# A pooling layer's channel product in three 16-bit products, with its weights in the common stream

## The chip, the cores and the metric

The kernel runs on one core of a Trainium2 chip. The metric is the device time of one execution in microseconds (us). Three runs of the kernel before gave 2080.56, 2081.57 and 2083.05 us, median 2081.57. The profiled execution took 2081.02 us, of which the span from the first to the last instruction is 2079.2 us.

The engines are called as the profile calls them: PE (matmul), PEld (weight load for PE), DVE (vector), ACT (scalar and activation), POOL, and SP (which issues nearly all DMA transfers). Each engine works through its own list of instructions in order, and waits where an instruction needs what another engine has not yet delivered.

## The reference, cut to what matters

Two layers work on 256 tokens of 2048 channels in 32-bit floats. Each layer has a token mixer and a gated FFN with a short convolution; each of the two is framed by RMS norms with shift, scale and gate. The mixer of layer 0 is a state-space layer with a GLU, that of layer 1 is a pooling mixer:

```python
def _pool_mixer(u, w, scale):
    ...
    for g, win in enumerate(POOL_WINDOWS):      # windows of 2, 4, 8, 16 tokens
        ...                                     # groups: 512 channels each
        groups.append((cs[:, hi + 1] - cs[:, lo]) / cnt - uf[:, :, ch])
    p = jnp.stack(groups, axis=2).astype(u.dtype)
    y = jnp.einsum("blgc,gcd->blgd", p, w).reshape(bsz, n_tok, dim)
    return y * scale
```

So each of four groups of 512 channels is averaged over a window of tokens (less the token itself) and multiplied by a matrix of 512 by 512. Both steps are linear, so that the kernel may multiply by the matrix first and pool afterwards.

## The kernel before, in words

Activations lie channel-major: `x` is 16 tiles of 128 channels by 256 tokens. The big products (GLU, FFN up, FFN down) are each made of three products of 16-bit halves, `hi*vh + hi*vl + lo*vh`, 256 tokens at a time. Their weights come as a stream of pieces of 128 by 2048 floats (`stream`, `self.pieces`). `load` brings piece q into one of three buffers `st`; `high` makes its 16-bit high part times 128 (`WS`) on ACT (`WH<-st` in the profile, L74); `ensure` then makes the low part on DVE (`XW<-st,WH`, L70), and issues the next load. High and low parts stand in a ring of four slots. I call high and low of one piece together a split. During the FFN, `after` keeps the splits three pieces ahead of the products. The order of every engine's work is that in which the Python code emits it.

Layer 1's mixer is emitted so. `norms(3)` sums the squares that the preceding FFN left and makes two row scales, `bc[0]` and `bc[1]`. `chain` then goes over the 16 tiles (two single ones, then seven pairs) on DVE: `op_t` scales the FFN's output (`Y<-Y,bc33bc`), `op_x` adds it to `x` (`XW<-XW,Y`), `op_r` scales `x` (`Z<-XW,mm33bc`), and ACT applies scale and shift. With `parted=False`, the pooling's call, the result stays a 32-bit tile `uf`; with `parted=True`, the FFN's call, ACT also writes the 16-bit high part and DVE, in `op_lo`, the low part (`Z<-u,Z`).

`pooling` works on four groups. `first(g)` multiplies tokens by the group's matrix: eight 32-bit products of 512 columns (`pp`), from weights that `pool_load` and one later transfer put into the buffer `G`; ACT copies the result out of PSUM. `second(g)` applies the pooling band (`py`, four output tiles of three small 32-bit products). For each output tile `sums` makes, on ACT, the scaled copy `Y<-py` and two squares `q<-py` and `q<-Y`, and on DVE a product `q<-Y,XW` and the running sum `G<-G,q` over 768 columns; there are three buffers `q`, and the last tile's sums are not added on DVE. The order is first(0), first(1), second(0), first(2), second(1), second(2), first(3), second(3). One piece of the stream is split meanwhile (`ensure(self.piece + 3)` after group 1); three more pieces, for the following FFN, have been split before the stage begins. `some()` slips in a little of a matrix-vector product (`gac`) for the conditioning.

Then `norms(3)` again, whose first matmuls (`pa`) need the running sum, and `ffn(1)`, whose first job `up_first` takes the tiles as `chain` delivers them (`pf`), the remaining jobs being `pu`.

Of the kernel before, what the change touches and what calls it, by code (L numbers as in the profile page):

```python
# [4 lines left out]
F32 = mybir.dt.float32  # L5
# [6 lines left out]
P = 128  # L12
# [33 lines left out]
class Net:  # L46
# [223 lines left out]
    def stream(self):  # L270
        A, half = self.A, lambda a: [a[:, :2048], a[:, 2048:]]
        self.pieces = []
        for i in range(NT):
            self.pieces += half(A["glu"][i])
        for l in range(2):
            a, b = half(A["up"][l, 0]), half(A["up"][l, 1])
            self.pieces += [a[0], b[0], a[1], b[1]]
            for i in range(2, NFF):
                self.pieces += half(A["up"][l, i])
            for j in range(NT):  # L280
                d = A["down"][l, j]
                self.pieces += [d[:, 0:2048], d[:, 2048:4096], d[:, 4096:5632]]
        self.piece = self.loaded = self.highs = self.lows = 0
        self.ring = [[t[:, i * 1024 : (i + 1) * 1024].bitcast(F16) for t in (self.WH, self.WL)] for i in range(4)]

        self.low0 = self.G[:, 10240:11264].bitcast(F16)
# [28 lines left out]
    def take(self):  # L315
        self.piece += 1
        return self.parts(self.piece - 1)[1:]
# [13 lines left out]
    def uh(self, k):  # L331
        return self.zh[k // 8][:, k % 8]
# [535 lines left out]
    def main(self):  # L868
        tc, nc, A = self.tc, self.nc, self.A
        par, con = self.par, self.con  # L870
        with tc.tile_pool(name="m1", bufs=1) as mp, tc.tile_pool(name="tm", bufs=2) as tm, tc.tile_pool(
# [10 lines left out]
            cvs = mp.tile([P, 2, 3, 88], F32, name="cvs")  # L882
            pcm = self.G[:, 11264 : 11264 + 8 * 4 + 8 * 64]
            load, high, ensure, take, prods, uh, ul = self.load, self.high, self.ensure, self.take, self.prods, self.uh, self.ul
            uf = self.Z.rearrange("p (k t) -> p k t", t=SEQ)

            cvf = cvs.rearrange("p l w t -> p (l w t)")
            nc.gpsimd.dma_start(pcm, A["pcm"])
# [217 lines left out]
                spread(1)  # L1106
                return bc

            def chain(bc, sh, parted=True):

                parts = [(0, 1), (1, 2)] + [(i, i + 2) for i in range(2, NT, 2)]
                tl = {}

                def op_t(a, b):
                    self.mul(ym[:, a:b], ym[:, a:b], bc[0][:, None, :].to_broadcast([P, b - a, SEQ]))

                def op_x(a, b):
                    self.add(x[:, a:b], x[:, a:b], ym[:, a:b])

                def op_r(a, b):  # L1120
                    t = uf[:, a:b]
                    if parted:
                        t = tl[a] = tm.tile([P, 2, SEQ], F32, tag="u", name=f"u{self.nq}_{a}", bufs=3)
                    self.mul(t[:, : b - a], x[:, a:b], bc[1][:, None, :].to_broadcast([P, b - a, SEQ]))
                    for i in range(a, b):
                        self.act(t[:, i - a], t[:, i - a], AF.Identity, vec[:, 1, i : i + 1], sh[:, i : i + 1])
                    if parted:
                        self.copy(self.zh[a // 8][:, a % 8 : a % 8 + b - a], t[:, : b - a])

                def op_lo(a, b):  # L1130
                    if not parted:
                        return
                    s = slice(a % 8, a % 8 + b - a)
                    self.sub(self.zl[a // 8][:, s], tl.pop(a)[:, : b - a], self.zh[a // 8][:, s])

                op_t(*parts[0])
                for s, ab in enumerate(parts):
                    op_x(*ab)
                    if s + 1 < len(parts):
                        op_t(*parts[s + 1])  # L1140
                    op_r(*ab)
                    if s:
                        op_lo(*parts[s - 1])
                        yield parts[s - 1][1]
                op_lo(*parts[-1])
                yield NT

# [88 lines left out]

            mem = [self.G[:, i * 2048 : (i + 1) * 2048] for i in range(5)]
            band = mem[3].rearrange("p (h g t) -> p h g t", h=2, g=4)
            wp = [mem[i].rearrange("p (k n) -> p k n", k=4) for i in (0, 1, 2, 1)]
            vts = [mem[i][:, j : j + 1024].rearrange("p (h n) -> p h n", h=2) for i in (4, 0) for j in (0, 1024)]  # L1240

            def pool_load():
                nc.sync.dma_start(mem[0], A["pool"][0])
                nc.sync.dma_start(mem[1], A["pool"][1])
                nc.sync.dma_start(mem[3], A["band"])
                nc.sync.dma_start(mem[2], A["pool"][2])

            def pooling(bc):
                need(8)
                self.mul(vec[:, 2], self.mod[:, 8, 0], par[:, Q_NG + 80 : Q_NG + 96])  # L1250
                self.mul(vec[:, 2], vec[:, 2], par[:, Q_PS : Q_PS + 16])
                out = chain(bc, self.mod[:, 6, 0], False)
                done = 0

                def ahead(n):
                    nonlocal done
                    while done < min(n, NT):
                        done = next(out)

                def first(g):  # L1260
                    ahead(4 * g + 4)
                    pv = [mps.tile([P, 512], F32, tag="mm", name=f"pp{g}_{h}") for h in range(2)]
                    for k in range(4):
                        for h in range(2):
                            self.mm(pv[h], uf[:, 4 * g + k, h * 128 : h * 128 + 128], wp[g][:, k], k == 0, k == 3)
                    if g == 1:
                        nc.sync.dma_start(mem[1], A["pool"][3])
                    ahead(8 if g == 0 else NT)
                    if g:
                        some()  # L1270
                        some()
                    if g == 1:
                        ensure(self.piece + 3)
                    for h in range(2):
                        self.copy(vts[g][:, h], pv[h])

                def second(g):
                    vt = vts[g]
                    for o in range(4):
                        ps = mps.tile([P, SEQ], F32, tag="mm", name=f"py{g}_{o}")  # L1280
                        for h, a, first, last in ((0, 120, True, False), (1, 120, False, True), (0, 0, True, True)):
                            t = slice(a, 256 if a else 120)
                            self.mm(ps[:, t], vt[:, h, o * 128 : o * 128 + 128], band[:, h, g, t], first, last)
                        i = g * 4 + o
                        fins.append(sums(3, i, ps, par[:, Q_PS + i : Q_PS + i + 1], vec[:, 2, i : i + 1], True))
                        if i < NT - 1:
                            step()

                first(0)
                first(1)  # L1290
                second(0)
                first(2)
                second(1)
                second(2)
                first(3)
                second(3)


            while self.loaded < self.lows + 3:
# [16 lines left out]
            scale(0, 2, 4)  # L1316
            bc = norms(4)
            ffn(0, bc, (1.4, 1.5))
            pool_load()
            need(7)  # L1320
            scale(1, 0, 1)
            bc = norms(3)
# [138 lines left out]
```

## Time and profile before

| | us |
|---|---|
| median of three runs | 2081.57 |
| profiled execution | 2081.02 |
| its span | 2079.2 |
| PE busy | 1907.9 (92%) |
| DVE busy | 1687.5 (81%) |
| ACT busy | 977.4 (47%) |
| pooling stage, from the chain's first DVE instruction to the norm's first `pa` | 46.88 |
| the norm behind it, `pa` to the first `pf` | 14.37 |
| `up_first` of layer 1, first `pf` to first `pu` | 24.07 |

A timeline row gives start, duration, engine, line, operation, output and inputs; in brackets stands how long the engine had been idle just before it, and which engine ended that. Durations overlap slightly, since an instruction begins before the one ahead of it has drained; the step from start to start is what a long row of instructions costs. The layer-1 pooling stage is only 2% of the span, so the averages of the whole page say little about it, and the rows below are taken from it.

### The profile page before, as it was taken

The page shows a single profiled execution, that of the slowest core. Times are in us where ns is not written, and L with a number is a line of the kernel's source. Part 1 is how long each engine was busy: PE and PEld are TensorE (multiplying, and loading weights), DVE is VectorE, ACT ScalarE, POOL GpSimd, SP SyncE. Part 2 cuts the span into 40 slices and gives each one's busy share as a digit, 9 for nine tenths or more (in the row PEclk, how much of TensorE's full clock was granted, in tenths as well). Part 3 has the DMA queues.
Part 4 walks back from the last instruction along what each step waited for, and adds up shares of the span by engine and source line. Part 5 has one row for each costly group of instructions (what it writes and reads, how often), then busy time and mean ns, then how long its engine had stood idle before and what let it go on. Part 6 is the DMA issues. An engine that isn't in the chain of part 4 may idle for free. (4 is left out here: it accounts for less than half of the span.)

```text
span 2079.2 us, 44155 instructions
## 1 busy us (share of the span) xinstructions
PE 1907.9 (92%) x19300; PEld 1624.0 (78%) x19300; DVE 1687.5 (81%) x2204; ACT 977.4 (47%) x1139; POOL 111.6 (5%) x129
## 2 busy tenths in 40 slices
PE   5773775799989999999999999889999999999998
PEld 3651552688878888888888888578888888888886
DVE  8799889699889999999998898878777766654444
ACT  2341651655555554554444443655545555543442
POOL 0440251200000000000000000000000000000000
PEclk9785897899989999999999999889999999999999
DMA  8565347599938999999999999327767656555652
GB/s 320 223 237 215 138 179 264 217 356 367 334 111 335 340 355 341 333 338 328 343 332 357 358 366 353 137 100 264 259 236 261 242 201 203 198 190 201 209 201 77
DMA packets 77585, 541.62 MB, mean 260 GB/s; under 512 B 8912, under 2 KB 9168, under 8 KB 16464
## 3 DMA queue, kind: packets, MB, share of 16 engines
q1 hardware_dynamic: 74304, 526.06, 69.1%
q0 software_dynamic: 3088, 12.74, 1.6%
q8 instruction: 151, 2.47, 0.5%
q14 instruction: 42, 0.34, 0.0%
HBM read 536.67 MB, written 2.10 MB: 259 GB/s over the span
## 5 line engine op out<-in xcount | busy, mean ns | idle before, releaser
L82 PEld LDWEIGHTS <-WH 128*128 128x128 f16 x9472 | 927.3, 98 | 118.7 <-issue 9.5
L70 DVE SCALAR_TENSOR_TENSOR XW<-st,WH 128x2048 f16<-128x2048 f32 (+1 forms) x303 | 676.2, 2233 | 276.3 <-ACT WH L74 275.8
L74 ACT ACTIVATE WH<-st 128x2048 f16<-128x2048 f32 (+1 forms) x304 | 566.7, 1865 | 704.8 <-PE pu L82 364.4
L82 PE MATMUL pu<-Z,WH 128*128 128x256 f16 x5376 | 881.2, 273 | 0.0
L82 PE MATMUL pu<-Z,XW 128*128 128x256 f16 x2688 | 732.7, 273 | 0.0
L82 PEld LDWEIGHTS <-XW 128*128 128x128 f16 x4720 | 462.6, 98 | 59.6 <-issue 3.4
L82 PE MATMUL pd<-G,WH 128*128 128x256 f16 x2816 | 461.8, 273 | 0.2 <-DVE G L52 0.2
L82 PE MATMUL pd<-G,XW 128*128 128x256 f16 x1408 | 383.8, 273 | 0.0
L70 DVE SCALAR_TENSOR_TENSOR gac<-ra,cpad,gac 128x1024 f32<-128x1024 f32 x128 | 163.9, 1280 | 3.2 <-DMA ra<-ada 1.8
L82 PE MATMUL pg<-Z,WH 128*128 128x256 f16 x960 | 157.5, 273 | 0.0
L70 DVE SCALAR_TENSOR_TENSOR gac<-st,cpad,gac 128x1024 f32<-128x1024 f32 x112 | 143.4, 1281 | 7.3 <-DMA st<-ada 5.8
L70 DVE SCALAR_TENSOR_TENSOR hc<-pu,cvs,hc 128x255 f32<-128x255 f32 x336 | 138.6, 475 | 0.6 <-ACT hc L76 0.6
L82 PE MATMUL pg<-Z,XW 128*128 128x256 f16 x480 | 130.8, 273 | 1.6 <-DVE XW L70 1.6
L82 PE MATMUL gv<-st,cpad 128*32 128x128 f32 (+2 forms) x1024 | 87.7, 476 | 45.4 <-DMA st<-ada 45.4
L82 PEld LDWEIGHTS gv<-st,cpad 128*32 128x32 f32 x1024 | 30.9, 128 | 76.5 <-DMA st<-ada 60.7
L76 ACT ACTIVATE hc<-pu,par,cvs 128x256 f32<-128x256 f32 x168 | 84.3, 551 | 8.0 <-DVE G L52 8.0
L82 PE MATMUL y<-G,QX 128*32 128x128 f32 x768 | 32.0, 302 | 39.1 <-ACT QX L74 37.9
L82 PEld LDWEIGHTS y<-G,QX 128*32 128x32 f32 x768 | 23.9, 122 | 42.5 <-ACT QX L74 39.4
L52 DVE TENSOR_TENSOR G<-G,q 128x768 f32<-128x768 f32 (+2 forms) x56 | 49.8, 890 | 5.5 <-ACT q L74 3.6
L74 ACT ACTIVATE QX<-XW 64x512 f32<-64x512 f32 x32 | 35.7, 1116 | 36.3 <-DVE XW L52 30.3
L82 PE MATMUL pf<-Z,WH 128*128 128x256 f16 x256 | 47.7, 291 | 5.4 <-ACT Z L74 3.2
L74 ACT ACTIVATE hc<-hc 128x256 f32<-128x256 f32 x88 | 35.6, 405 | 27.7 <-DVE hc L70 26.4
(231 smaller groups left out, 1511.9 us busy)
## 6 DMA issues: line engine op xcount, KB each, us to landing
st<-up SPq DMA_DIRECT2D x176, 1024.0 KB, 6.2
st<-ada SPq DMA_DIRECT2D x128, 1024.0 KB, 6.8
ra<-ada SPq DMA_DIRECT2D x64, 1024.0 KB, 7.2
st<-down SPq DMA_DIRECT2D x64, 1024.0 KB, 5.1
st<-glu SPq DMA_DIRECT2D x32, 1024.0 KB, 7.5
st<-down SPq DMA_DIRECT2D x32, 768.0 KB, 5.3
Cz<-cz POOLq DMA_DIRECT2D x16, 256.0 KB, 5.3
G<-pool SPq DMA_DIRECT2D x4, 1024.0 KB, 8.5
```

The lines of the kernel that those rows point to most:

```text
L52: self.nc.vector.tensor_tensor(out=out, in0=a, in1=b, op=op)
L70: self.nc.vector.scalar_tensor_tensor(out, a, s, b, op0, op1)
L74: self.nc.scalar.activation(out, a, f, scale=scale)
L76: self.nc.scalar.activation(out, a, f, bias=bias, scale=scale)
L82: self.nc.tensor.matmul(out, l, r, start=start, stop=stop)
```

## The change

The four matrices of the pooling layer become pieces of the stream, behind the first FFN's last weights; `pool_load` is gone, and only the band has a transfer of its own. `chain` always makes 16-bit high and low parts. `first` makes each 32-bit product out of three 16-bit ones (96 of 512 columns in all in place of 32 in 32 bits), as the tiles come, and its copies divide by 128. `first(3)` moves ahead of `second(2)`. Splits of pieces stand at other places: two after group 2, one after `second(2)`, one after `second(3)` has been emitted.

```diff
+            if l == 0:
+                self.pieces += [A["pool"][g] for g in range(4)]
...
-                    t = uf[:, a:b]
-                    if parted:
-                        t = tl[a] = tm.tile([P, 2, SEQ], F32, tag="u", name=f"u{self.nq}_{a}", bufs=3)
+                    t = tl[a] = tm.tile([P, 2, SEQ], F32, tag="u", name=f"u{self.nq}_{a}", bufs=3)
...
                 def first(g):
-                    ahead(4 * g + 4)
+
                     pv = [mps.tile([P, 512], F32, tag="mm", name=f"pp{g}_{h}") for h in range(2)]
+                    hi, lo = (t.rearrange("p (k n) -> p k n", k=4) for t in take())
                     for k in range(4):
+                        i = 4 * g + k
+                        ahead(i + 1)
                         for h in range(2):
-                            self.mm(pv[h], uf[:, 4 * g + k, h * 128 : h * 128 + 128], wp[g][:, k], k == 0, k == 3)
-                    if g == 1:
-                        nc.sync.dma_start(mem[1], A["pool"][3])
-                    ahead(8 if g == 0 else NT)
+                            vh, vl = (v[:, h * 128 : h * 128 + 128] for v in (uh(i), ul(i)))
+                            self.mm(pv[h], vh, hi[:, k], k == 0, False)
+                            self.mm(pv[h], vh, lo[:, k], False, False)
+                            self.mm(pv[h], vl, hi[:, k], False, k == 3)
+                    ahead(4 * g + 8)
                     if g:
                         some()
                         some()
-                    if g == 1:
-                        ensure(self.piece + 3)
                     for h in range(2):
-                        self.copy(vts[g][:, h], pv[h])
+                        self.copy(vts[g][:, h], pv[h], 1.0 / WS)
+                    if g > 1:
+                        ensure(self.piece + 3 - g)
...
                 second(0)
                 first(2)
                 second(1)
+                first(3)
                 second(2)
-                first(3)
+                ensure(self.piece + 1)
                 second(3)
+                ensure(self.piece + 2)
...
-            pool_load()
+            nc.sync.dma_start(mem[3], A["band"])
```

What that does to the order on DVE and ACT is seen at three places. First, DVE at the end of the chain, around the first sums (`u` and `Z` are the tiles of the chain, `gac` the matrix-vector product, `G` the running sum). Before:

```order
L52 TENSOR_TENSOR XW<-XW,Y 128x512
L52 TENSOR_TENSOR Z<-XW,mm33bc 128x512
L65 TENSOR_SCALAR gac<-st_71,cpad 128x1024
L70 SCALAR_TENSOR_TENSOR XW<-st_68,WH 128x2048
L70 SCALAR_TENSOR_TENSOR G<-Y,XW 128x256
L70 SCALAR_TENSOR_TENSOR q_14114<-Y,XW 128x256
```

In the changed kernel:

```order
L65 TENSOR_SCALAR gac<-st_71,cpad 128x1024
L70 SCALAR_TENSOR_TENSOR G<-Y,XW 128x256
L70 SCALAR_TENSOR_TENSOR q_14158<-Y,XW 128x256
L52 TENSOR_TENSOR G<-G,q_14158 128x768
L70 SCALAR_TENSOR_TENSOR q_14167<-Y,XW 128x256
L52 TENSOR_TENSOR XW<-XW,Y 128x512
L52 TENSOR_TENSOR u_14_14208<-XW,mm33bc 128x512
L52 TENSOR_TENSOR Z<-u_12_14133,Z 128x512
L52 TENSOR_TENSOR Z<-u_14_14208,Z 128x512
L52 TENSOR_TENSOR mod<-gm_13324,par 128x16
L70 SCALAR_TENSOR_TENSOR gac<-st_71,cpad,gac 128x1024
L70 SCALAR_TENSOR_TENSOR XW<-st_68,WH 128x2048
```

The last pair's three steps, two low parts and the first split now stand behind the first sums; a second split (`XW<-st_69,WH`) follows directly.

Second, DVE near the end of the stage, where the last running sums stand ahead of the norm (`sa<-pa`). Before:

```order
L70 SCALAR_TENSOR_TENSOR q_14261<-Y,XW 128x256
L70 SCALAR_TENSOR_TENSOR vec<-mod,par 128x16
L52 TENSOR_TENSOR G<-G,q_14261 128x768
L70 SCALAR_TENSOR_TENSOR q_14271<-Y,XW 128x256
L52 TENSOR_TENSOR G<-G,q_14271 128x768
L70 SCALAR_TENSOR_TENSOR q_14297<-Y,XW 128x256
L65 TENSOR_SCALAR sa_14280<-pa_14290 128x6
```

In the changed kernel:

```order
L70 SCALAR_TENSOR_TENSOR q_14354<-Y,XW 128x256
L70 SCALAR_TENSOR_TENSOR XW<-st_68,WH 128x2048
L70 SCALAR_TENSOR_TENSOR vec<-mod,par 128x16
L52 TENSOR_TENSOR G<-G,q_14354 128x768
L70 SCALAR_TENSOR_TENSOR q_14364<-Y,XW 128x256
L52 TENSOR_TENSOR G<-G,q_14364 128x768
L70 SCALAR_TENSOR_TENSOR q_14393<-Y,XW 128x256
L65 TENSOR_SCALAR sa_14376<-pa_14386 128x6
```

The fourth split now stands ahead of the last two running sums; the third stands four outputs earlier in the same way.

Third, ACT at the same place, where the fourth split's high part is. Before:

```order
L74 ACTIVATE Y<-py_2_14265,vec 128x256
L74 ACTIVATE q_14271<-py_2_14265,par 128x256
L74 ACTIVATE q_14271<-Y 128x256
L74 ACTIVATE Y<-py_3_14275,vec 128x256
L74 ACTIVATE q_14297<-py_3_14275,par 128x256
```

In the changed kernel:

```order
L74 ACTIVATE Y<-py_2_14358,vec 128x256
L74 ACTIVATE q_14364<-py_2_14358,par 128x256
L74 ACTIVATE q_14364<-Y 128x256
L74 ACTIVATE WH<-st_68 128x2048
L74 ACTIVATE Y<-py_3_14368,vec 128x256
L74 ACTIVATE q_14393<-py_3_14368,par 128x256
```

The high part of a piece that only the following FFN reads now stands between the third and the last output of group 3.

## Rows read from the trace of the kernel before

**Rows 1.** Chain of waits, 1300 to 1367 us: start, us, what.

```profile
1306.48 15.81 PE pp L82 x32
...
1337.83 6.89 PE pp L82 x16
...
1350.12 0.97 DVE G L52
...
1351.13 2.72 PE pa L82 x12
```

**Rows 2.** Stages: length; busy PE, PEld, DVE, ACT, POOL; clock, DMA share, GB/s.

```profile
1304.25:1351.13 46.88, 42.21 (x168) 24.93 (x167) 38.94 (x64) 32.11 (x74) 0.00 (x0) 0.94 0.27 109
...
1389.73:1830.00 440.27, 440.27 (x4040) 393.60 (x4038) 323.98 (x372) 227.05 (x257) 0.00 (x0) 1.00 0.68 236
```

**Rows 3.** DVE groups, 1304.2 to 1351.5 us: busy, mean ns, idle before.

```profile
L52 DVE TENSOR_TENSOR G<-G,q 128x768 f32<-128x768 f32 x14 | 13.4, 958 | 1.6 <-ACT q L74 0.7
L70 DVE SCALAR_TENSOR_TENSOR q<-Y,XW 128x256 f32<-128x256 f32 x15 | 6.3, 421 | 3.7 <-ACT Y L74 3.7
...
L70 DVE SCALAR_TENSOR_TENSOR gac<-st,cpad,gac 128x1024 f32<-128x1024 f32 x1 | 1.3, 1276 | 0.0
```

**Rows 4.** DVE timeline of the pooling stage.

```profile
1305.04 0.41 DVE L52 TENSOR_TENSOR Y<-Y,bc33bc 128x256 f32<-128x256 f32 x1
1305.38 0.41 DVE L52 TENSOR_TENSOR Z<-XW,mm33bc 128x256 f32<-128x256 f32 x1
...
1317.16 0.68 DVE L52 TENSOR_TENSOR Z<-XW,mm33bc 128x512 f32<-128x512 f32 x1
1317.76 0.69 DVE L52 TENSOR_TENSOR XW<-XW,Y 128x512 f32<-128x512 f32 x1
...
1319.08 0.75 DVE L65 TENSOR_SCALAR gac<-st,cpad 128x1024 f32<-128x1024 f32 x1
1322.39 2.29 DVE L70 SCALAR_TENSOR_TENSOR XW<-st,WH 128x2048 f16<-128x2048 f32 x1 [2.56 <-ACT WH L74]
1324.60 0.42 DVE L70 SCALAR_TENSOR_TENSOR G<-Y,XW 128x256 f32<-128x256 f32 x1
...
1333.57 0.43 DVE L70 SCALAR_TENSOR_TENSOR q<-Y,XW 128x256 f32<-128x256 f32 x1 [3.07 <-ACT Y L74]
```

**Rows 5.** ACT timeline: a high part, copies, one output tile, a low-part pair.

```profile
1320.46 1.90 ACT L74 ACTIVATE WH<-st 128x2048 f16<-128x2048 f32 x1
1322.26 1.06 ACT L74 ACTIVATE G<-pp 128x512 f32<-128x512 f32 x2
...
1334.10 0.47 ACT L74 ACTIVATE Y<-py,vec 128x256 f32<-128x256 f32 x1
...
1335.12 0.49 ACT L74 ACTIVATE Y<-py,vec 128x256 f32<-128x256 f32 x1
...
1375.85 0.63 ACT L74 ACTIVATE Z<-u 128x512 f16<-128x512 f32 x1
```

**Rows 6.** DVE timeline of the FFN's chain, layer 1.

```profile
1362.67 0.42 DVE L52 TENSOR_TENSOR Y<-Y,bc50bc 128x256 f32<-128x256 f32 x1
...
1383.24 0.69 DVE L52 TENSOR_TENSOR Z<-u,Z 128x512 f16<-128x512 f32 x1 [1.22 <-ACT Z L74]
```

**Rows 7.** PE timeline of `up_first`: layer 1 (from 1365), layer 0 (from 588).

```profile
1365.50 0.89 PE L82 MATMUL pf<-Z,WH 128*128 128x256 f16 x2 [1.59 <-ACT Z L74]
...
1389.57 0.38 PE L82 MATMUL pu<-Z,WH 128*128 128x256 f16 x2
...
588.12 0.89 PE L82 MATMUL pf<-Z,WH 128*128 128x256 f16 x2 [1.59 <-ACT Z L74]
...
601.00 0.27 PE L82 MATMUL pf<-Z,WH 128*128 128x256 f16 x1 [1.82 <-DVE Z L52]
...
613.99 0.38 PE L82 MATMUL pu<-Z,WH 128*128 128x256 f16 x2
```

**Rows 8.** DVE timeline of the FFN's chain, layer 0.

```profile
596.26 2.29 DVE L70 SCALAR_TENSOR_TENSOR XW<-st,WH 128x2048 f16<-128x2048 f32 x1
```

More of the change, by code (lines that the diff above doesn't have):

```diff
@@ L884, in main @@
             load, high, ensure, take, prods, uh, ul = self.load, self.high, self.ensure, self.take, self.prods, self.uh, self.ul
-            uf = self.Z.rearrange("p (k t) -> p k t", t=SEQ)
             cvf = cvs.rearrange("p l w t -> p (l w t)")
@@ L1107, in norms, with chain @@
                 return bc
-            def chain(bc, sh, parted=True):
+            def chain(bc, sh):
                 parts = [(0, 1), (1, 2)] + [(i, i + 2) for i in range(2, NT, 2)]
@@ L1126, in op_r @@
                         self.act(t[:, i - a], t[:, i - a], AF.Identity, vec[:, 1, i : i + 1], sh[:, i : i + 1])
-                    if parted:
-                        self.copy(self.zh[a // 8][:, a % 8 : a % 8 + b - a], t[:, : b - a])
+                    self.copy(self.zh[a // 8][:, a % 8 : a % 8 + b - a], t[:, : b - a])
                 def op_lo(a, b):
-                    if not parted:
-                        return
                     s = slice(a % 8, a % 8 + b - a)
@@ L1238, in main @@
             band = mem[3].rearrange("p (h g t) -> p h g t", h=2, g=4)
-            wp = [mem[i].rearrange("p (k n) -> p k n", k=4) for i in (0, 1, 2, 1)]
             vts = [mem[i][:, j : j + 1024].rearrange("p (h n) -> p h n", h=2) for i in (4, 0) for j in (0, 1024)]
[L1242 to L1246, printed above, removed]
             def pooling(bc):
@@ L1251, in pooling @@
                 self.mul(vec[:, 2], vec[:, 2], par[:, Q_PS : Q_PS + 16])
-                out = chain(bc, self.mod[:, 6, 0], False)
+                out = chain(bc, self.mod[:, 6, 0])
                 done = 0
```

## The prediction

> **What bounds the kernel now.** I read the chain of waits first. In the pooling stage it is nearly all PE: 15.81 us of `pp`, then twice 16 instructions in about 6.9 us, the short `py` between, and only at the end ACT and DVE, up to the running sum after which PE starts `pa` [rows 1]. By that view the 32-bit products are the bound. The busy times of the stage say more: of 46.88 us PE is busy 42.2 and DVE 38.9 [rows 2], so DVE comes close behind. Then the groups of DVE show what its waits are: 3.7 us ahead of `q<-Y,XW` and 0.7 us ahead of `G<-G,q`, both for ACT [rows 3], one of them 3.07 us at 1333.57, while DVE has nothing to do because PE is still in `pp` [rows 4]. So a PE gain is worth little here unless DVE has room, and whatever is added to DVE's list uses that room up at once. Last, the stage behind: from 1389.73 PE is busy all 440.27 us of the next window, at a granted clock of 1.00, which is its level of 2.4 GHz [rows 2]. What the pooling stage loses, nothing there gives back.
>
> **PE.** Two 32-bit instructions make one product of 512 columns: eight products in 6.89 us, 0.86 us each [rows 1]. 16-bit matmuls of 256 columns cost 440.27 us / 4040 = 0.109 us [rows 2]; one of 512 columns is not in the trace, and I estimate it at 0.218 us, three at 0.65. The whole of `pp` then is 96 times 0.218, about 21 us at full clock. The nearest row is better: `up_first` has the same columns (192 of 256), the same chain and the same start after a norm, and takes 24.07 us [rows 7]; before, `pp` takes 15.8 + 6.9 + 6.9 = 29.6. PE has 5.5 us less to do.
>
> **DVE up to the first sum.** Each engine works in order, so I follow DVE's list. Nothing ahead of 1304.25 changes: the three pieces split in advance have the same size, whether they belong to the pool or to the FFN. A chain step costs 0.34 us for one tile and 0.60 for a pair [rows 4]. Ahead of the first sum the changed list has 8 single and 24 pair steps: 8 x 0.34 + 24 x 0.60 = 17.1 us, and 0.7 for `gac`, which ends at 1322.1. The first sum needs ACT: the last pair step that scales `x` starts 1.2 ahead of the chain's end, at 1320.2, and ends at 1320.8; then come two shifts of about half a microsecond and the 16-bit copy (0.63), two copies of `pp` (1.06) and a `Y`, with a small copy of 0.3 between [rows 5]. That makes 1324.5. PE is not late: half of 24 us, and the slow start, bring it to `py` at about 1321. In the kernel before the same instruction starts at 1324.60 [rows 4]. So the first sum starts when it did.
>
> **DVE from there to `pa`.** Before, 26.5 us remain (1324.60 to 1351.13) [rows 1, 4]. To these the change adds what stood ahead of the first sum or did not stand in the stage: two steps of the last pair and two low parts, 4 x 0.60 = 2.4 us, and four splits. A split is 2.21 us on DVE (1322.39 to 1324.60) [rows 4]; four are 8.84. (Before, one split stood ahead of that sum, partly in time in which DVE waited anyway.)
>
> Waits: the 4.4 us for ACT [rows 3] go, since ACT is ahead of DVE from now on. In their place come four. The chain's last low part waits for ACT's copy, as it does in the FFN's chain, 1.22 us [rows 6]. The first split's high part stands behind two copies (1.06 + 1.90 = 2.96 us [rows 5]), while DVE has 0.60 + 0.1 + 1.2 of work [rows 3, 4]: 1.1 us of wait. The third and the fourth split each wait about 0.9: ACT may write squares only three tiles ahead, as DVE frees a buffer; from that point ACT needs two squares and the high part, 0.7 + 1.9 us (an output of three costs 1.02 [rows 5]), and DVE gets there after 1.4 + 0.35. The second split's high part is ready. Together 4.1 us, 0.3 less than what goes. The stage so ends 2.4 + 8.84 - 0.3 = 10.9 us later, and `pa` starts at about 1362.
>
> Both ends of the disputed part: with no wait at all DVE still has 2.4 + 8.84 - 4.4 = 6.8 us more; with the high part of each split wholly in series (1.81 us each, the step of rows 5, where I count 2.9 for all) it is 10.9 + 7.2 - 2.9 = 15.2. I take 10.9, as every one of its waits has a row.
>
> **The FFN behind.** Before, its first four pieces are split when the FFN starts. Now three are, and the fourth's split falls into the chain, as in layer 0, where DVE does one at 596.26 [rows 8]. There PE then waits 1.82 us, and `up_first` takes 613.99 - 588.12 = 25.87 us against 24.07 in layer 1 [rows 7]. I take +1.8; it could be 0 (PE starts slowly and so has work in hand) or the whole split, 2.2. After that both kernels hold the same pieces.
>
> **What is free.** The pool's four transfers move into the stream, early; the band stays one transfer, behind fewer. In the stage the DMA share is 0.27 [rows 2]; if a transfer came late, a split would wait for it, but pieces are loaded three ahead, 10 us and more. The copies' division costs nothing, being an operand of the same instruction. ACT's eight to nine more copies and three more high parts, about 10 us on 32.1 busy of 46.88 [rows 2], hide beside DVE's 10.9. That first(3) stands earlier takes away PE's wait for its copy, which is not late any more.
>
> **Sum.** The profiled execution took 2081.0 us, 0.55 under the median of 2081.57. 2081.0 + 10.9 + 1.8 = 2093.7 us.
>
> **Rivals.** (1) PE stays the bound, and the change gains. Then 5.5 us go from `pp`, 0.6 come back since the first product waits for the extra copy (1365.50 - 1362.67 = 2.83 us after the chain's start, against 2.23) [rows 1, 2, 6, 7], and 1.8 in the FFN: 2077.9 us. It decides if the last output of `second(3)` reaches DVE after DVE's list has run dry. For it speaks the chain of waits; against it that DVE has 8 us of idle time in the stage and gets 11.5 of work: nine low parts (4.9) and three splits more (6.6). Chance 0.05.
> The Trainium skill, page "FP8 and Floating Point Precision", section "TensorE Precision Notes", says that a true 32-bit product takes four passes through the array; by it, three 16-bit passes save a quarter of 27.5 us, 6.9, and with no other term the time would be 2074. The trace agrees on the four (0.86 against 0.218), and says that this stage doesn't end on them.
>
> (2) Lost and found: DVE has all its waits removed, the FFN's chain keeps its 24.07, and the tail behind the last sum shortens. 2081.0 + 6.8 = 2087.8, at best about 2085, which would be within 0.2% (4.2 us, about what a measurement of this kernel can tell from no change). It needs ACT to be ahead at every split; the three `q` buffers speak against it. Chance of a time within 0.2%: 0.07, the rest of this case counts as slower.
>
> (3) ACT and DVE alternate at the splits in full, 15.2 us, and the FFN's chain loses 2.2: 2098.4 us. For it: the high parts stand in ACT's list among outputs that DVE must free first. Against it: DVE has one to two microseconds of sums to do meanwhile. Chance 0.12.
>
> (4) The pieces of the pool are not ready when `first` takes them, so that the change does not work as a stream. Against it: three are split before the stage begins, and the fourth ahead of first(3) by ten instructions of DVE. Its price is small, as PE has slack. Chance 0.02, inside the range.
>
> My forecast has 0.74. Faster 0.05, same 0.07, slower 0.88. The range goes from 2086.5 (under the case with no waits) to 2098.5 (the case with all of them).
>
> **What would show it.** `pa` of the second norm at about 1362 in place of 1351.13, the first sum of the stage still near 1324.5, four splits of 2.2 us on DVE between there and `pa`, short DVE waits for `WH` ahead of three of them, and none of 3 us for `Y`. `pp` of about 0.22 us a matmul, PE's idle time in the stage well above the 4.7 us of before. In `up_first` a wait of nearly 2 us for DVE. Wrong I would be if DVE waited for `Y` near the stage's end, or if ACT were so late that the sums wait for it.

## The result, and the profile after

The changed kernel takes 2098.14 us (median of 4 runs, 2096.87 to 2098.83) against 2081.98 (4 runs of the kernel before on the same chip): ratio 1.0076, 95% interval 1.0064 to 1.0089. It is slower by three quarters of a per cent. The forecast was 2093.7 with a range of 2086.5 to 2098.5.

The profiled execution took 2096.87 us with a span of 2095.1, which is 15.9 longer than before. First the stages (length; busy time of PE, PEld, DVE, ACT, POOL with instruction counts; granted clock; DMA share; GB/s): the pooling stage, the norm behind it, `up_first`.

```profile
1304.62:1365.32 60.70, 37.18 (x200) 23.41 (x200) 50.53 (x76) 43.20 (x86) 0.00 (x0) 0.84 0.23 75
1365.32:1379.64 14.32, 7.67 (x32) 7.05 (x33) 9.21 (x48) 1.02 (x2) 0.00 (x0) 0.50 0.12 51
1379.64:1405.51 25.87, 23.89 (x192) 19.91 (x192) 22.78 (x33) 18.82 (x27) 0.00 (x0) 0.89 0.13 43
```

Against [rows 2] the stage is 13.82 us longer, though PE is busy 5.0 less; DVE is busy 11.6 more. The norm kept its length (14.32 against 14.37), `up_first` lost 1.80, and from there to the end both kernels take the same (689.59 and 689.63). Another 0.37 us lie ahead of the stage, in unchanged code. So the whole loss is in two places, 13.8 and 1.8 us.

The chain of waits of the stage (start, length, what) was PE's for most of its length in [rows 1]. Now it is DVE's up to 1321.32, then ACT's, then PE's from 1323.40 to 1333.72, and from the first split on that of DVE and ACT:

```profile
1323.07 0.28 ACT gr L74
1323.40 0.82 PE gm L82 x4
1324.21 4.29 PE py L82 x24
1328.50 5.19 PE pp L82 x24
1333.72 0.60 ACT G L74
1334.32 1.81 ACT WH L74
...
1351.64 1.81 ACT WH L74
1353.47 2.29 DVE XW L70
...
1358.77 1.81 ACT WH L74
1360.60 2.29 DVE XW L70
...
1365.32 2.69 PE pa L82 x12
```

The first split waits for ACT's high part, which stands behind PE's products and their copies; the last two splits, ACT's high part and then DVE's low part, stand in the chain that leads to `pa`. The DVE groups of the stage (busy, mean ns, idle before) answer to [rows 3]:

```profile
L70 DVE SCALAR_TENSOR_TENSOR XW<-st,WH 128x2048 f16<-128x2048 f32 x4 | 9.1, 2290 | 3.3 <-ACT WH L74 3.3
L70 DVE SCALAR_TENSOR_TENSOR q<-Y,XW 128x256 f32<-128x256 f32 x15 | 6.3, 418 | 0.9 <-ACT Y L74 0.9
L70 DVE SCALAR_TENSOR_TENSOR G<-Y,XW 128x256 f32<-128x256 f32 x1 | 0.4, 425 | 3.7 <-ACT Y L74 3.7
```

The wait of 3.7 us for ACT's `Y` ahead of the products `q` is down to 0.9, but 3.7 us of such a wait stand ahead of the first sum, where DVE waited 2.56 us for `WH` before [rows 4]; and 3.3 us of wait for `WH` have come. Where they stand, the DVE timeline shows, against [rows 4]:

```profile
1326.28 0.42 DVE L70 SCALAR_TENSOR_TENSOR G<-Y,XW 128x256 f32<-128x256 f32 x1 [3.73 <-ACT Y L74]
1327.61 0.42 DVE L70 SCALAR_TENSOR_TENSOR q<-Y,XW 128x256 f32<-128x256 f32 x1 [0.91 <-ACT Y L74]
1328.28 0.96 DVE L52 TENSOR_TENSOR G<-G,q 128x768 f32<-128x768 f32 x1 [0.24 <-ACT q L74]
...
1332.72 0.69 DVE L52 TENSOR_TENSOR Z<-u,Z 128x512 f16<-128x512 f32 x1 [1.22 <-ACT Z L74]
...
1336.15 4.49 DVE L70 SCALAR_TENSOR_TENSOR XW<-st,WH 128x2048 f16<-128x2048 f32 x2 [1.46 <-ACT WH L74]
...
1353.47 2.29 DVE L70 SCALAR_TENSOR_TENSOR XW<-st,WH 128x2048 f16<-128x2048 f32 x1 [0.91 <-ACT WH L74]
...
1360.60 2.29 DVE L70 SCALAR_TENSOR_TENSOR XW<-st,WH 128x2048 f16<-128x2048 f32 x1 [0.91 <-ACT WH L74]
```

From the first sum on, that is 1326.28, DVE waits 0.91 + 0.24 + 1.22 + 1.46 + 0.91 + 0.91 = 5.65 us; the rest of that stretch of 39.04 us is work without a gap. ACT, for its part, waits for DVE to free `q` buffers and then puts the high part between two outputs, as its timeline shows, against [rows 5]:

```profile
1325.77 0.47 ACT L74 ACTIVATE Y<-py,vec 128x256 f32<-128x256 f32 x1 [1.45 <-PE py L82]
...
1356.67 0.47 ACT L74 ACTIVATE q<-py,par 128x256 f32<-128x256 f32 x1 [1.83 <-DVE G L52]
```

Last the PE timeline: around the first `py`, at the stage's end, and in `up_first`, against [rows 7].

```profile
1323.40 0.82 PE L82 MATMUL gm<-con,gr 128*128 128x8 f32 x4 [3.54 <-ACT gr L74]
1324.07 4.44 PE L82 MATMUL py<-G 128*128 128x136 f32 x24
...
1333.52 2.90 PE L82 MATMUL py<-G 128*128 128x136 f32 x24
...
1365.32 2.69 PE L82 MATMUL pa<-con,G 128*128 128x1 f32 x12 [15.78 <-DVE G L52]
...
1392.53 0.27 PE L82 MATMUL pf<-Z,WH 128*128 128x256 f16 x1 [1.82 <-DVE Z L52]
```

PE stands idle 15.78 us ahead of `pa`. And the first `py` starts late: `gm`, a tiny matmul of the matrix-vector product, waits for a small ACT copy (`gr`) that stands behind ACT's work on the sixth pair. Then it runs slowly, at a mean granted clock of 0.65 (columns as in the first table):

```profile
1323.40:1328.30 4.90, 4.90 (x28) 4.90 (x29) 0.87 (x3) 3.26 (x9) 0.00 (x0) 0.65 0.00 0
```

### The profile page after: what moved, and what is told of

Read it like the earlier page. It is cut to its first block, busy times and chain, and to the rows that moved or that the text cites. A ratio compares the mean times of both kernels' runs of the same rounds, so it can differ in the third digit from the quotient of the medians.

```text
span 2095.1 us, 44243 instructions
## 1 busy us (share of the span) xinstructions
PE 1901.2 (91%) x19332; PEld 1625.1 (78%) x19332; DVE 1700.7 (81%) x2217; ACT 990.8 (47%) x1152; POOL 103.4 (5%) x129
## 5 line engine op out<-in xcount | busy, mean ns | idle before, releaser
L70 DVE SCALAR_TENSOR_TENSOR XW<-st,WH 128x2048 f16<-128x2048 f32 (+1 forms) x307 | 685.2, 2233 | 272.2 <-ACT WH L74 271.8
L74 ACT ACTIVATE WH<-st 128x2048 f16<-128x2048 f32 (+1 forms) x308 | 574.1, 1865 | 696.3 <-PE pu L82 353.7
L82 PE MATMUL gv<-st,cpad 128*32 128x128 f32 (+2 forms) x1024 | 81.4, 449 | 50.4 <-DMA st<-ada 50.4
L76 ACT ACTIVATE u<-u,mod,vec 128x256 f32<-128x256 f32 x48 | 26.5, 593 | 53.8 <-DVE u L52 53.8
```

Of the source, the lines that this page charges most:

```text
L70: self.nc.vector.scalar_tensor_tensor(out, a, s, b, op0, op1)
L74: self.nc.scalar.activation(out, a, f, scale=scale)
L76: self.nc.scalar.activation(out, a, f, bias=bias, scale=scale)
L82: self.nc.tensor.matmul(out, l, r, start=start, stop=stop)
```

## The experiments

The instructions of the first 1300 us are the same in all kernels but e9 and e10, which change layer 0's FFN chain too, yet their length differed by up to 10 us between runs (the stage began at 1301.6 to 1311.2). The experiments are therefore read from the trace, from the chain's first DVE instruction on; what follows `up_first` took 689.6 to 689.9 us in every one. Stage, norm and `up_first` are as defined in the table of before; the times are medians of up to 12 runs (two in e1, e3 and e4), and each ratio is against runs of the kernel before taken beside them, whose medians were 2081.0 to 2083.6.

| kernel | stage | norm | up_first | sum | time | ratio (95%) |
|---|---|---|---|---|---|---|
| before | 46.88 | 14.37 | 24.07 | 85.32 | 2081.98 | |
| after | 60.70 | 14.32 | 25.87 | 100.89 | 2098.14 | 1.0076 (1.0064 to 1.0089) |
| e1_four_products | 60.85 | 14.32 | 25.87 | 101.04 | 2096.06 | 1.0070 (1.0047 to 1.0092) |
| e2_norm_splits | 54.76 | 14.33 | 25.86 | 94.95 | 2090.14 | 1.0048 (1.0032 to 1.0064) |
| e3_gr_early | 59.87 | 14.34 | 25.86 | 100.07 | 2099.09 | 1.0084 (1.0064 to 1.0104) |
| e4_low_on_pool | 56.65 | 14.39 | 25.86 | 96.90 | 2096.34 | 1.0071 (1.0050 to 1.0092) |
| e5_all | 51.79 | 14.38 | 25.87 | 92.04 | 2090.71 | 1.0028 (1.0013 to 1.0043) |
| e6_no_split_in_sums | 43.89 | 29.37 | 24.16 | 97.42 | 2099.17 | 1.0056 (1.0036 to 1.0076) |
| e7_before_split_away | 47.04 | 14.25 | 23.28 | 84.57 | 2084.69 | 0.9993 (0.9976 to 1.0011) |
| e8_old_order | 60.83 | 14.36 | 25.88 | 101.07 | 2100.21 | one run |
| e9_splits_out_low_on_pool | 44.07 | 14.38 | 29.09 | 87.54 | 2083.18 | 1.0008 (0.9996 to 1.0021) |
| e10_before_low_on_pool | 47.61 | 13.73 | 23.65 | 84.99 | 2081.44 | 0.9995 (0.9985 to 1.0006) |

The stage falls into two parts at the start of its first split among the sums. For the kernels that have one there, in us from the stage's start:

| kernel | first sum | first split | DVE's wait for its `WH` | from the first split to `pa` | splits in that part |
|---|---|---|---|---|---|
| after | 21.66 | 31.53 | 1.46 | 29.17 | 4 |
| e1_four_products | 20.77 | 31.66 | 2.78 | 29.19 | 4 |
| e2_norm_splits | 20.88 | 31.54 | 2.23 | 23.22 | 2 |
| e3_gr_early | 20.49 | 30.68 | 2.08 | 29.19 | 4 |
| e4_low_on_pool | 18.30 | 27.46 | 3.49 | 29.19 | 4 |
| e5_all | 18.29 | 28.55 | 4.59 | 23.24 | 2 |
| e8_old_order | 20.87 | 31.55 | 2.26 | 29.28 | 4 |

In these kernels the second part depends on its splits alone. The first part ends each time when ACT's high part is ready, and DVE has waited for it.

**More work for PE: e1_four_products.** A fourth 16-bit product (low by low) is added to every product of `first`.

```diff
-                            self.mm(pv[h], vl, hi[:, k], False, k == 3)
+                            self.mm(pv[h], vl, hi[:, k], False, False)
+                            self.mm(pv[h], vl, lo[:, k], False, k == 3)
```

> The changed kernel with a fourth 16-bit product (low part of the activations times low part of the weights) in the pooling layer: 32 more matmuls of 512 columns on PE, 32 x 0.216 = 6.9 us, and nothing on any other engine. Theory (DVE's list ends the stage, PE has slack): the products of groups 0 and 1 end 3.5 us later, which is inside the 3.54 us that PE waits there for ACT's copy of the matrix-vector rows; those of group 2 end 1.7 us later, and ACT's copies of them stand ahead of the first high part, so that DVE's first split starts up to 1.7 us later; the last group hides. In all +0 to +2 us, 2098 to 2100. Rival (PE's products set the length of the stage): +6.9 us, 2105.

Its stage (columns as above):

```profile
1301.61:1362.46 60.85, 42.68 (x233) 25.33 (x232) 50.55 (x76) 43.23 (x86) 0.00 (x0) 0.84 0.22 75
```

its `gm` and first `py`, and DVE at the first split:

```profile
1320.55:1323.75 3.20, 3.20 (x30) 3.19 (x30) 0.76 (x2) 2.67 (x8) 0.00 (x0) 1.00 0.00 0
1333.27 4.49 DVE L70 SCALAR_TENSOR_TENSOR XW<-st,WH 128x2048 f16<-128x2048 f32 x2 [2.78 <-ACT WH L74]
```

PE is busy 5.5 us more, and the stage is 0.15 longer, so rival (1), in which the stage ends on PE, is out. But the small number is a balance of two. `gm` starts as late as in the changed kernel (18.94 us after the stage's start, 18.78 there), yet PE has worked up to it, its granted clock is 1.00 in place of 0.65, and `gm` and `py` take 3.2 us in place of 4.9. Then the third group of products has 32 matmuls in place of 24, 1.73 us more at 0.216 each. ACT's copies and the first high part follow, so that the first split starts 0.13 us later, and DVE, whose first sum came 0.89 us sooner, waits 1.32 us longer for it. So ahead of the first split PE's time does count. (Four products of 0.216 us are 0.86, as much as a 32-bit product before. The Trainium skill, page "FP8 and Floating Point Precision", section "TensorE Precision Notes", lets a 32-bit product cost four passes; this agrees.)

**The splits among the sums: e2_norm_splits.** The third and fourth split move into the norm, where DVE waits for PE.

```diff
+                if fill:
+                    self.high(self.piece + 2)
+                    ensure(self.piece + 1)
...
+                pq = total(self.last_q, "pq")
+                if fill:
+                    ensure(self.piece + 2)
...
                 second(2)
-                ensure(self.piece + 1)
                 second(3)
-                ensure(self.piece + 2)
```

> The changed kernel with its third and fourth split moved out of the sums: their high parts stand on ACT behind the stage, their low parts on DVE in the following norm, where DVE waits 2.54 us for the first column sums and 2.19 us for the second. Theory: each split costs 2.21 us on DVE and 0.91 us of waiting for ACT, so the norm's first matmul starts 2 x 3.12 = 6.2 us earlier (1359.1 in place of 1365.3), and the norm itself gets at most 0.3 us longer: 2092 us. Rival (the stage ends on PE or ACT, and DVE only shows it): no change, 2098. Second rival (DVE is bound, but what is taken out of the sums comes back in the norm): 2096 to 2098 with an earlier first matmul and a longer norm.

The DVE timeline of its norm:

```profile
1357.91 2.29 DVE L70 SCALAR_TENSOR_TENSOR XW<-st,WH 128x2048 f16<-128x2048 f32 x1
1360.53 0.17 DVE L65 TENSOR_SCALAR sa<-pa 128x6 f32<-128x6 f32 x1 [0.34 <-PE pa L82]
...
1360.81 2.29 DVE L70 SCALAR_TENSOR_TENSOR XW<-st,WH 128x2048 f16<-128x2048 f32 x1
```

The stage shrinks by 5.94 us and the norm keeps its 14.33: two splits of 2.21 with a wait of 0.91 each are 6.24. In the norm they are free, since DVE would wait for `pa` and `pq` anyway. The edit takes the high parts out of ACT's list as well, so that it does not separate the two engines; the rows give 2.21 us of DVE's work and 0.91 of waiting for ACT to each split.

**The late first sum: e3_gr_early.** The rest of the chain that `first(g)` emits moves behind the matrix-vector work, so that the copy `gr` stands earlier in ACT's list.

```diff
-                    ahead(4 * g + 8)
                     if g:
                         some()
                         some()
+                    ahead(4 * g + 8)
```

> The changed kernel with the two slots for the matrix-vector product in group 1 moved ahead of the chain's next tiles, so that ACT's copy of its rows doesn't stand behind two pairs of the chain, and PE doesn't wait 3.54 us for it ahead of the first pooling products. Theory: the first sum starts at about 1324.5 in place of 1326.28, and PE doesn't fall to the lower clock there, so that the second sum loses its 0.91 us of wait as well: -2 to -2.5 us, 2096. Rival (the first sum waits for ACT's copies of the products, not for PE): 0 to -0.5 us.

PE's timeline there:

```profile
1322.10 0.51 PE L82 MATMUL gm<-con,gr 128*128 128x8 f32 x4
1322.46 2.30 PE L82 MATMUL py<-G 128*128 128x136 f32 x18
```

`gm` no longer waits, the first 18 `py` run at the quick pace (24 would take 3.1 us), and the first sum comes 20.49 us after the stage's start, against 21.66 and, in the kernel before, 20.35. Only 0.83 of the 1.17 us reach the stage's end, less than half of what I expected. With this order the last pair stands behind `gac` (1.28 us) in DVE's list, ACT's work on that pair and the high part come behind it, and DVE waits 2.08 us for the first `WH` in place of 1.46.

**DVE's chain: e4_low_on_pool.** The nine low parts of the pooling chain go to POOL.

```diff
+                gsub = lambda o, a, b: nc.gpsimd.tensor_tensor(out=o, in0=a, in1=b, op=OP.subtract)
+                out = chain(bc, self.mod[:, 6, 0], gsub)
```

> The changed kernel with the nine low parts of the pooling chain made on POOL in place of DVE. Theory (DVE's list is the bound): DVE loses 4.9 us; of that 1.2 us and the 1.22 us of wait for ACT stand behind the first sum and count in full, the rest lets the chain end up to 3.6 us earlier, and counts as far as the first sum then starts earlier (up to 2 us, since ACT and PE follow): -2.5 to -4.5 us, 2094 to 2096, if POOL keeps up (its 32-bit operation of 256 columns takes about 1 us, a pair would take 2, against 2.6 us of PE work per pair). Rival (POOL is slower than that, or slows DVE down while it works): 0 to +5 us, with PE waiting for POOL in the products.

The group on POOL, from the lines of the stage:

```profile
L1241 POOL TENSOR_TENSOR Z<-u,Z 128x512 f16<-128x512 f32 x7 | 9.7, 1384 | 11.4 <-ACT Z L74 8.8 <-DVE u L52 2.6
```

and PE's `gm` and DVE's first split:

```profile
1325.82 0.61 PE L82 MATMUL gm<-con,gr 128*128 128x8 f32 x4 [0.78 <-ACT gr L74]
...
1336.92 4.49 DVE L70 SCALAR_TENSOR_TENSOR XW<-st,WH 128x2048 f16<-128x2048 f32 x2 [3.49 <-ACT WH L74]
```

DVE's busy time falls by 4.95 us (50.53 to 45.58) and the stage by 4.05. That the two are close does not mean that DVE's work came back nearly in full. `gm` starts 16.36 us after the stage's start in place of 18.78: 2.4 us come from DVE's shorter chain. PE waits 0.78 us for it and not 3.54, its granted clock is then 1.00 in place of 0.65, and from the start of `gm` to that of the first high part 9.27 us pass in place of 10.92: that is the other 1.65. The low parts taken away behind the first sum bring nothing, since DVE waits 3.49 us for the first `WH` in place of 1.46. The time over all shows little of it (1.0071), as the part ahead of the stage was 4.8 us longer in its profile.

**All three: e5_all.** e2, e3 and e4 together.

> The changed kernel with three edits at once: third and fourth split in the norm, the matrix-vector slots ahead of the chain's next tiles, and the nine low parts on POOL. Alone they shortened the stretch from the chain's first DVE instruction to the FFN's first job behind up_first by 5.94, 0.82 and 3.99 us, from 100.89. Theory (all three take work or waits off one and the same list, DVE's): they add up, 10.7 us, so 90.2 us for that stretch, and about 2087 us in time. Rival (once DVE is relieved, ACT or PE ends the stage): a stretch of 92 to 95, with DVE waiting for Y near the stage's end.

ACT ahead of its first splits, and DVE at them:

```profile
1326.32 1.09 ACT L76 ACTIVATE u<-u,mod,vec 128x256 f32<-128x256 f32 x2 [1.97 <-DVE u L52]
...
1330.87 4.50 DVE L70 SCALAR_TENSOR_TENSOR XW<-st,WH 128x2048 f16<-128x2048 f32 x2 [4.59 <-ACT WH L74]
```

Singly the three give 5.94 + 0.83 + 4.05 = 10.82 us, together 8.91. DVE reaches the first split sooner than ACT has made its high part, and stands there 4.59 us. ACT in turn has waited 1.97 us for DVE's `u` of the last pair, which stands behind `gac` as in e3. So with low parts on POOL the order of e3 does harm: the first split starts 1.09 us later than in e4.

**No split among the sums: e6_no_split_in_sums.** Of the four splits one moves ahead of the first sums (its high part into the norm in front), two into the norm behind. The fourth, and the one in `up_first`'s chain, are left to POOL in that norm, with two instructions each for a low part. Low parts of the pooling chain on POOL and the early `gr` are kept.

```diff
+            if pool:
+                self.nc.gpsimd.tensor_scalar(w, w, WS, None, OP.mult)
+                self.nc.gpsimd.tensor_tensor(out=lo, in0=w, in1=hi, op=OP.subtract)
...
+                if fill == 2:
+                    ensure(self.piece + 1)
+                    ensure(self.piece + 3, True)
```

> The same with no split left among the sums: the pool's last matrix has its high part made in the norm ahead of the stage and its low part on DVE where DVE waits for the first sum; of the FFN's four first pieces two have their low parts in the two waits of the norm behind the stage, and two on POOL (a multiplication by 128 in place and a subtraction). Theory: of the 90.2 us expected of the three edits go one split in the sums with its share of waiting (2.2 to 3.5 us) and the split in up_first with PE's wait of 1.8 us: 84.8 to 86.2, as in the kernel before (85.32), and 2080 to 2083 us, within a measurement's reach of it. That would say that what the change lost was where the splits and low parts stand, and that the 5.5 us that PE saves are nearly used up by the chain's low parts and the first sum. Rival (PE's gain is now free): 80 to 82 us, 2077. Second rival: POOL is too slow for its two splits (more than 24 us for both), and up_first waits for it.

The stage came down to 43.89 us, 2.99 under the kernel before, and `up_first`, with all four pieces ready, to 24.16: so the 1.8 us of `up_first` belong to the split in its chain. But the norm took 29.37 us, and the sum of 84.8 to 86.2 that I expected was missed by far. POOL's timeline in it:

```profile
1358.04 7.16 POOL L315 TENSOR_SCALAR st<-st 128x2048 f32<-128x2048 f32 x1 [20.00 <-ACT WH L74]
1365.29 4.06 POOL L316 TENSOR_TENSOR XW<-st,WH 128x2048 f16<-128x2048 f32 x1
1369.33 5.36 POOL L315 TENSOR_SCALAR st<-st 128x2048 f32<-128x2048 f32 x1
1374.77 4.06 POOL L316 TENSOR_TENSOR XW<-st,WH 128x2048 f16<-128x2048 f32 x1
```

and DVE's, where each of these instructions has one or two columns:

```profile
1360.17 5.07 DVE L65 TENSOR_SCALAR rt<-sa 128x2 int32<-128x2 int32 x1
...
1365.84 3.59 DVE L70 SCALAR_TENSOR_TENSOR rw<-rt,rw 128x1 f32<-128x1 f32 x2
...
1369.77 3.26 DVE L70 SCALAR_TENSOR_TENSOR rw<-rt,rw 128x1 f32<-128x1 f32 x2
...
1375.79 3.06 DVE L65 TENSOR_SCALAR rt<-msx 128x2 int32<-128x2 int32 x1
```

Elsewhere they take 0.17 and 0.28 us. Three of the four end within 0.1 us of the end of a POOL instruction (1365.20, 1369.35, 1378.83). The four lose 14.1 us, which is the norm's loss of 15.0 but for one.

**The kernel before with the same freedom: e7_before_split_away.** The one split in the stage of the kernel before moves into the norm.

```diff
-                    if g == 1:
-                        ensure(self.piece + 3)
...
+                if fill:
+                    ensure(self.piece + 3)
```

> The kernel before with its only split in the pooling stage moved into the following norm's first wait: 2.21 us less for DVE and 1.81 less for ACT in the stage. Theory (there PE's 32-bit products end the stage, DVE has room): no change, -0.3 to +0.2 us in the stage of 46.88 us. Rival (DVE's list is the bound before as well): -2.2 us. Beside the split taken out of the changed kernel's sums, which was worth 3 us, this tells whether the bound has changed from PE to DVE.

Its stage (columns as above):

```profile
1311.15:1358.19 47.04, 42.36 (x168) 25.01 (x167) 36.77 (x63) 31.35 (x74) 0.00 (x0) 0.93 0.22 83
```

and the DVE groups that wait in it (busy, mean ns, idle before):

```profile
L70 DVE SCALAR_TENSOR_TENSOR G<-Y,XW 128x256 f32<-128x256 f32 x1 | 0.4, 426 | 4.3 <-ACT Y L74 4.3
L70 DVE SCALAR_TENSOR_TENSOR q<-Y,XW 128x256 f32<-128x256 f32 x15 | 6.3, 421 | 4.3 <-ACT Y L74 4.3
```

DVE does 2.2 us less, and the stage is as long as it was; DVE waits 4.3 us for `Y` ahead of the first sum, where it waited 2.56 for `WH` and then made the split, and 0.6 more later. In the kernel before this split was free; in the changed one each of the last two costs about 3 us (e2). The places differ, ahead of the first sum and among the last ones; what they show together is that before DVE had room in the stage, and now has none where the splits stand. (The 0.79 us that `up_first` is shorter goes with the granted clock: 0.58 in its first 3.5 us and 1.00 in the next 6, against 0.50 and 0.78. So differences of that size between kernels can come from the clock.)

**The order: e8_old_order.** `first(3)` goes back behind `second(2)`.

```diff
                 second(1)
-                first(3)
                 second(2)
-                ensure(self.piece + 1)
+                ensure(self.piece + 2)
+                first(3)
                 second(3)
```

> The changed kernel with first(3) back behind second(2), as it was before the change; the third split stays behind second(2). PE and ACT have slack there, DVE's list keeps its order. Theory (DVE is the bound): -0.3 to +0.5 us. Rival (ACT is the bound at the end of the stage): up to 1.1 us longer, since the two copies of the last product then stand between the outputs of groups 2 and 3, with PE's wait for them.

60.83 us against 60.70: the reordering neither costs nor brings anything.

**Towards a better version: e9_splits_out_low_on_pool.** e6 with the two splits of POOL made on DVE, in the chain of `up_first`; low parts of all chains on POOL.

```diff
+                    nc.gpsimd.tensor_tensor(out=self.zl[a // 8][:, s], in0=tl.pop(a)[:, : b - a], in1=self.zh[a // 8][:, s], op=OP.subtract)
...
+                if fill == 2:
+                    ensure(self.piece + 1)
```

> The changed kernel with no split among the sums, as in the run without them, but nothing long on POOL: the FFN's first two pieces have their low parts in the two waits of the norm, the next two on DVE in up_first's chain, and the low parts of all three chains (pooling and both FFNs) are made on POOL. Theory (DVE's list was the bound, and what blocked DVE in the norm of that run was POOL's long operations on whole pieces): a stage of about 44 us, a norm of 14.4, an up_first of layer 1 of 24 to 26 us (two splits more on DVE, nine low parts fewer), together 82.5 to 84.5 against 85.32 before the change; layer 0's up_first goes from 25.87 to about 24.1. In time 2076 to 2080, below the kernel before. Rival (DVE is blocked whenever POOL works, whatever the operation's length): a chain step of DVE beside POOL's gets longer, 86 or more, 2083 and up.

The norm is back at 14.38, which shows that it was POOL's long instructions that blocked DVE in e6. The stage keeps its gain (44.07), and with DVE relieved its chain of waits is PE's again, from `pp` on:

```profile
1310.03 12.42 PE pp L82 x46
...
1333.56 5.18 PE pp L82 x24
```

But `up_first` takes 29.09, as two timelines show: DVE's, in a pair step behind a split,

```profile
1375.31 1.63 DVE L52 TENSOR_TENSOR XW<-XW,Y 128x512 f32<-128x512 f32 x1
```

and PE's:

```profile
1376.45 0.37 PE L82 MATMUL pf<-Z,WH 128*128 128x256 f16 x1 [2.95 <-POOL Z L1142]
```

The 2.8 us gained in the stage against the kernel before are outweighed by 5.0 lost there; in layer 0, whose FFN chain has its low parts on POOL as well, `up_first` takes 25.01 us in place of 25.87. The time equals that of the kernel before, and misses the 2076 to 2080 that I expected; sum and time are those of the rival (86 or more, 2083 and up), though of DVE's pair steps in `up_first` only two are longer (1.65 and 1.63 us), and not each one beside POOL, as the rival has it.

**The rest of that without the change: e10_before_low_on_pool.** The kernel before, with the FFN chains' low parts on POOL (the same edit of `chain` alone).

> The kernel before with only the low parts of the two FFN chains made on POOL; its pooling stage has none. It tells how much of the last run's gain has nothing to do with 16-bit pooling products. Theory: layer 0's up_first loses PE's wait of 1.82 us for DVE (25.87 to about 24.1), layer 1's, which PE bounds (24.07), stays, and so does the pooling stage (46.88): -1.5 to -2 us. Rival (POOL is late with the low parts): both get longer.

Layer 0's `up_first` takes 24.51 us in place of 25.87 (about 24.1 expected). Layer 1's gains 0.42 us, the stage loses 0.73 at a lower granted clock (0.92 against 0.94), the sum gains 0.33; over all no difference can be told. No version that ran beats the kernel before by more than its measurement can tell.

## Why the prediction was right, and where it was not

- **The bound passes to DVE.** Right in the main. From the first split to `pa` every kernel with four splits takes 29.2 us, and two splits fewer give 5.95 back (e2). In the kernel before the split in the stage was free (e7). Ahead of the first split it holds in part: there the chain goes through DVE's tiles, ACT's copy `gr`, PE's `gm`, `py` and `pp`, and ACT's copies and high part (e1, e3, e4).
- **The terms 2.4 and 8.84.** From the first sum to `pa` 39.04 us against 26.53, 12.51 more. Less the change in waits (5.65 that came, 4.4 that went) this leaves 11.26, and 2.4 + 8.84 is 11.24.
- **The waits, "together 4.1 us".** Mis-sized: they are 5.65. Their places were the predicted ones, at 1.22 (said 1.22), 1.46 (1.1), 0.91 and 0.91 (0.9 each). Missing were 0.91 + 0.24 us at the first sums, where ACT still follows PE's slow first `py`; I had said that ACT is ahead from then on.
- **"So the first sum starts when it did."** Wrong by 1.31 us, counted from the stage's start (21.66 against 20.35). I followed ACT's copies and held PE for ready, and passed over the `gm` that stands ahead of the first `py` in PE's list: it waits for `gr`, a copy behind ACT's work on the sixth pair. Of the 1.31, 0.89 is PE's slow pace behind that wait (e1 starts `gm` as late, without the pause). The wait of 3.73 us for `Y` ahead of this sum is one of the kind that the signs excluded ("none of 3 us"). These two misses, 1.55 + 1.31, are the 2.9 us by which the stage's loss of 13.8 passes the 10.9 of the sum.
- **Where the 2.9 us lie.** All ahead of the first split. By the terms of the forecast it starts 28.7 us after the stage's start (20.35, then 6.04 of DVE's work as measured, 1.22 and 1.1 of waits); it starts at 31.53. From there to `pa` the forecast leaves 29.1, and 29.17 were measured. It is not the first sum that decides: in e8, with the same code up to there, the sum comes at 20.87 and the split at 31.55. The step that failed is that I put ACT's first high part behind two copies only, and held PE, which these copies wait for, for ready: `py` was to start at about 1321 and started at 1324.07.
- **`up_first`, +1.8.** Right: 25.87 against 24.07, with the wait of 1.82 us; e6 takes it away.
- **PE 5.5 us less.** 5.0 measured, at a lower mean clock (0.84 in the stage, 0.94 before). A 16-bit product of 512 columns steps by 0.216 us in the quick part of `pp`, against the 0.218 of the estimate.
- **What was called free** was: no split of the stage waits for a transfer, and the order of `first(3)` does nothing (e8).

In all 10.9 + 1.8 = 12.7 was forecast and 15.6 measured in the two stages; 0.37 us more came ahead of them in the profiled execution, and the median of the runs is 1.3 above that execution. That 2098.14 still lies in the range, by 0.36 us, is luck: its upper end was made for rival (3). The median falls next to the time of rival (3), 2098.4; but its mechanism, in which ACT's high part and DVE's low part of each split stand fully in series, is not what ran: the two late splits wait 0.91 us each and not 1.8.

## What to carry to other kernels

Before making the busiest engine cheaper, compare it with the second busiest in the same stage: here 42.2 against 38.9 us of 46.9 left room for a little, and a cheaper form that needs 11 us more of the second engine puts 50.5 us of its work into that stage, and loses unless work moves elsewhere (e9's stage, with DVE at 41.2, took 44.07). A split, a copy or a conversion has a price that depends on the place: the same 2.2 us of DVE were free in a norm that waits for PE, cost 1.8 in a chain that feeds PE, and about 3 among sums that have to wait for ACT as well. And when the first output of a stage is timed, every small instruction ahead of it in each engine's list belongs to the path, with what it waits for.

## What was not expected of the hardware

- **Long POOL instructions stop DVE.** While POOL worked on 128x2048 floats, DVE instructions of one or two columns took 5.07, 3.59, 3.26 and 3.06 us in place of 0.17 to 0.28 (e6; the second and third figure are pairs). The Trainium skill, page "GPSIMD Engine Reference", section "1. Specifications", says that POOL shares its interfaces to SBUF with VectorE and contends with DVE instructions that have two SBUF inputs or run in a 2-port mode. The trace agrees that they contend; two of the four have a single input, and no run shows the mode in which they ran. Three of the four end with a POOL instruction, so that DVE waited for the whole rest of it, which a chain of short dependent instructions pays several times over. With 128x512 on POOL the price was about 1 us at a time (a pair step of 1.63 us in place of 0.68 in e9).
- **PE comes back slowly.** After 3.54 us of idle time 24 `py` took 4.44 us, against 2.90 for the next 24. The granted clock accounts for it: from 1324.4 to 1326.4 it was 0.50, the level of 1.2 GHz, and from 1327.4 on 1.00, that of 2.4 GHz. The 4.90 us of `gm` and `py` at a mean of 0.65 are 3.2 us at 1.00, which is what e1 takes for them at 1.00. ACT is not the brake, since it waits for `py` (1.45 us ahead of the first `Y`). e3 has the quick pace in its first 18 `py`, then waits 1.92 us for ACT, and its granted clock in the 4 us behind that is 0.58.
